# Buffers of the seven-product units in the place of the norms' tiles, half of the residual added on VectorE, and a finish without GpSimd

## The chip, the cores and the metric

The kernel runs on one core of a Trainium2 chip. The engines of the core work side by side, each in its own program order: TensorE multiplies (PE for the matmuls, PEld for its weight loads), VectorE (DVE), ScalarE (ACT) and GpSimd (POOL) work on tiles, and SyncE (SP) issues most of the transfers (DMA). An engine waits at an instruction until what that instruction needs is there, and everything behind it waits as well. The metric is the time of one execution on the device, in microseconds (us).

## The reference, cut to what matters

One layer of a trunk over 512 rows of 2048 values: normalise, project, mix, project back, add; then a feed-forward part with a convolution and a gate, and add again. What the change touches is the second and the third line.

```python
mixed = concatenate([y_sb, y_df, y_lru, y_sc], axis=-1) @ w_out[l]
x = x + rms_norm(mixed, norm_gains[l, 1])
h = rms_norm(x, norm_gains[l, 2])
u = causal_dwconv(h @ w_up, conv_w)          # three taps along the rows
g, up = split(u, 2, axis=-1)                 # 4096 columns each
x = x + rms_norm((gelu(g) * up) @ w_down, norm_gains[l, 3])
```

## The kernel before

Everything lies transposed: 128 partitions of columns, and the 512 rows run along the free axis in two halves of 256. Every float32 operand is split into a high and a low part, and a product is the sum of three (high by high, high by low, low by high). A weight tile of 128x1024 (512 KB) is loaded on SP's queue into a `w_raw` buffer, cast to `w_hi` on ACT, and its remainder `w_lo` is formed on DVE. That is `chunk` (lines 97 to 100) for the plain products, and `raw` (L993) with `operand` (L999, L1000) for the units below. TensorE needs one such tile about every 2.9 us.

The stages up to about 710 us (the input projection and the four mixers) are not touched. Then come:

- **The output projection** (`out_group`). Its last two groups of columns are worked for each half of the rows, first half 0, then half 1. When the last group of a half is done, `residual(hf)` is called a few ticks later. A tick is a piece of some four to eight matmuls, and `at` hangs work on a later tick.
- **`residual(hf)`** multiplies the projected values in `mg` by the norm's factor in eight operations on DVE (L833), and lets GpSimd add them to `x` with four transfers that accumulate in place (L834, `xs<-mg`, 512 KB each, q = 0 to 3).
- **`squares(hf, q)`** squares the new x on ACT (L844), sums on DVE (L846), writes the values scaled by the gains (L848) and stores x for later on SP's queue (L850, `x1_d`). Hung on ticks 22, 25, 28 and 31 after the residual; `norm2` on tick 42.
- **`norm2(hf)`** sums over the partitions with two matmuls on TensorE (L857, they read `s` from L846), and normalises and splits the result.
- **`up_plain`**: the first four pairs of column blocks of the up projection as plain products, each 128x514 row buffer `ub` (zeroed in its first two columns, L926) filled from PSUM, then convolved (`conv`: L939 on ACT, two taps L941 on DVE, into an `f2` tile) and gated (`glu`, L949).
- **`up_unit`**, 28 units (4 to 31), from about 865 to 1427 us. Each makes one pair of blocks from seven products instead of eight (a Strassen-like scheme): `product` (L1013 high, L1018 low) multiplies eight tiles of 128x512 and eight of 128x256. Sums of weight blocks are made by accumulating transfers of GpSimd (L1033), or on DVE in unit 4 (`add`, L1005). `keep` (L1028 on ACT, L1029 on DVE) and `add_result` (L1024) move PSUM results into `ug` and `uv`, the unit's two `ub` buffers. A PSUM tile is free for its next product when `keep` has read it.
- **The down projection**, and **`finish(hf)`** for each half: eight pairs of a multiplication by the factor (L1133) and an addition of the stored x (L1135). For half 1 four of the eight additions are on GpSimd, whose results leave by ACT's queue; the rest leaves by SP's.

Buffers: the pool `ph2` holds the norms' tiles; `t2f` has six `f2` tiles and `ubp` eight `ub` tiles, and all units share them with `up_plain`. The order of each engine's instructions is set by a scheduler; work under `high_priority` is put ahead of what stands later in the program.

Of the kernel before, what the change touches and what calls it, by code (L numbers as in the profile page):

```python
# [9 lines left out]
F32 = mybir.dt.float32  # L10
# [6 lines left out]
P = 128  # L17
# [31 lines left out]
def trunk(ctx: ExitStack, tc: tile.TileContext, xT, params, consts, wgate, w_in, w_out, w_up0, w_up, w_dn, out):  # L49
# [57 lines left out]
    def at(block, fn):  # L107
        assert block >= clock[0], (block, clock[0])
        beside.setdefault(block, []).append(fn)
# [662 lines left out]
    with ExitStack() as ph:  # L772
        wide = ph.enter_context(tc.tile_pool(name="wide", bufs=2))
        ystage = ph.enter_context(tc.tile_pool(name="ystage", bufs=3))
        up_ph = ph.enter_context(ExitStack())
        ph2 = up_ph.enter_context(tc.tile_pool(name="ph2", bufs=1))
        t2p = up_ph.enter_context(tc.tile_pool(name="t2f", bufs=6))
        ubp = up_ph.enter_context(tc.tile_pool(name="ubp", bufs=8))

        def t2(dt=F32):  # L780
            return t2p.tile([P, S], dt, name="f2")
# [43 lines left out]
        def residual(hf):  # L825

            ts = HALVES[hf]
            ss1[hf].rstd(rstd1[:, ts])
            acc = ph2.tile([P, 2, S // 2], F32, name="s2")
            for q in range(4):  # L830
                for i in range(2):
                    m = mg[q][hf][:, 2 * i:2 * i + 2]
                    V.tensor_tensor(out=m, in0=m, in1=repeated(rstd1[:, ts], 2), op=ALU.mult)  # L833
                G.dma_start(out=xs[q][hf], in_=mg[q][hf], accum_op=ALU.add)  # L834
                at(clock[0] + 22 + 3 * q, lambda q=q: squares(hf, q, acc))
            at(clock[0] + 42, lambda: norm2(hf, acc))

        def squares(hf, q, acc):

# [12 lines left out]
        def norm2(hf, acc):  # L852

            ts = HALVES[hf]
            ps = mm_tile()[:, 0:S // 2]
            for i in range(2):
                T.matmul(ps, lhsT=ones, rhs=acc[:, i], start=i == 0, stop=i == 1)  # L857
            with tc.high_priority(offset=AHEAD):
                rstd_of(ps, D, rstd2[:, ts], t1)
            for k in range(0, KT, 2):  # L860
                ks = slice(k % 4, k % 4 + 2)
                h = mg[k // 4][hf][:, ks]
                V.tensor_tensor(out=h, in0=h, in1=repeated(rstd2[:, ts], 2), op=ALU.mult)
                split(h, actq[k // 4][:, 0, ks, ts], actq[k // 4][:, 1, ks, ts])
            if hf == 1:
                sums_of_h()
# [59 lines left out]
            V.memset(t[:, 0:2], 0.0)  # L926
            return t

        neg_w = ph2.tile([P, 96], F32, name="neg_w")
        fw = PC["ffn_w"]  # L930
        V.tensor_scalar(out=neg_w, in0=par[:, fw + 96:fw + 192], scalar1=-1.0, scalar2=0.0,
                        op0=ALU.mult, op1=ALU.add)
# [42 lines left out]


        split_t2()
        spare_t = wide.tile([P, 4, 4, S // 2], F32, name="mg")
        spare = [spare_t[:, i] for i in range(4)]
        turn = [0]  # L980
# [7 lines left out]
        def up_unit(unit):  # L988
# [51 lines left out]


            a11, a21 = raw(spare[n], 0, 0), raw(spare[2 + n], 1, 0)
            s3, a12, a22 = (by4(wp.tile([P, 2, S], F32, name="w_raw")) for _ in range(3))
            s1 = a21
            if unit == 4:
                add(s3, a11, a21)
# [77 lines left out]
        def finish(hf):  # L1124
            ts = HALVES[hf]
            ss3[hf].rstd(rstd3[:, ts])
            for n in range(KT // 2):
                ks = slice(2 * (n % 2), 2 * (n % 2) + 2)
                t = m3[n // 2][:, ks, ts]
                x1 = t2() if n % 2 == 0 else ystage.tile([P, S], F32, name="ys")  # L1130
                x1 = x1.rearrange("p (k t) -> p k t", k=2)
                nc.sync.dma_start(out=x1, in_=x1_d[n // 2][:, hf, ks])
                V.tensor_tensor(out=t, in0=t, in1=repeated(rstd3[:, ts], 2), op=ALU.mult)  # L1133
                pool = hf == 1 and n in (1, 3, 5, 6)
                (G if pool else V).tensor_tensor(out=x1, in0=t, in1=x1, op=ALU.add)  # L1135
                (nc.scalar if pool else nc.sync).dma_start(out=out[hf, n], in_=x1)

        for g in range(3):
            down_group(g, (0, 1), ALL, mm_tile if g % 2 == 0 else pa_tile)
# [113 lines left out]
```

## Time and profile before

| | before |
|---|---|
| median of 3 runs | 1803.43 us (1801.49 to 1803.82) |
| the profiled execution | 1803.49 us, of which the trace's span is 1801.8 |
| TensorE busy | 1754.5 us, 97% |
| VectorE busy | 1152.3 us, 64% |
| ScalarE busy | 868.9 us, 48% |
| GpSimd busy | 151.0 us, 8% |
| mean granted clock of TensorE | 0.989 |

TensorE is busy nearly everywhere, so what can be gained lies in the few places where it isn't: they are read from its timeline, where an idle stretch stands in brackets with the engine and the tile that ended it. Busy is not the same as fast: after a long pause the granted clock falls, and the same instructions take longer.

### The profile page before, as it was taken

What the parts mean: (1) busy time and instruction counts of PE and PEld (TensorE: products, weight loads), DVE (VectorE), ACT (ScalarE), POOL (GpSimd) and SP (SyncE); (2) the same over time, 40 slices, a digit from 0 to 9 for tenths busy, and PEclk for the clock granted to TensorE, in tenths of its full rate; (3) what the DMA queues carried; (4) which work ended last, traced back from release to release, by engine and by line L of the source; (5) the groups of instructions that cost most, each with busy time, mean ns of one, the idle gap of its engine ahead of it and who ended that gap; (6) DMA issues with size and microseconds to landing.
All of it is one profiled execution on the core that took longest, in us unless ns stands there. A gap on an engine that the chain in (4) does not pass through costs nothing.

```text
span 1801.8 us, 24904 instructions
## 1 busy us (share of the span) xinstructions
PE 1754.5 (97%) x9612; PEld 1524.1 (85%) x9612; DVE 1152.3 (64%) x1716; ACT 868.9 (48%) x1301; POOL 151.0 (8%) x215
## 2 busy tenths in 40 slices
PE   8999999999999999999799999999999999999995
PEld 7778788887888889999788888888888888888995
DVE  7884576566656224679888888888788852222364
ACT  6442676655334335667455455555555642122342
POOL 0000011100000111100011111111111001010101
PEclk9999999999999999999899999999999999999998
DMA  7224222242222635875788888888897773233465
GB/s 258 82 97 141 78 77 77 88 152 82 94 94 89 202 106 176 245 235 186 221 219 237 228 218 234 232 226 230 228 232 208 233 234 94 93 102 98 130 212 172
DMA packets 95726, 299.21 MB, mean 166 GB/s; under 512 B 10324, under 2 KB 14676, under 8 KB 95608
## 3 DMA queue, kind: packets, MB, share of 16 engines
q1 hardware_dynamic: 82072, 249.39, 42.3%
q0 software_dynamic: 12960, 47.19, 14.0%
q8 instruction: 75, 1.23, 0.3%
q10 hardware_dynamic: 576, 1.05, 0.2%
q14 instruction: 43, 0.35, 0.1%
HBM read 258.78 MB, written 21.24 MB: 155 GB/s over the span
## 4 chain that ended last, share of the span: by engine, by line
PE 90%; DVE 3%; issue 3%; DMA 2%; ACT 1%; POOL 0%; SPq 0%; ACTq 0%; POOLq 0%; DVEq 0%
PE mm L150 41%; PE mm L1013 20%; PE mm L1018 10%; PE pa L150 9%; PE mm L121 2%; PE mm L123 2%; PE mm L122 2%; PE pa L575 1%; DMA w_raw<-in_w_out_dram 1%; DMA xs<-mg 1%; DMA w_raw<-in_w_up_dram 1%; DVE f L941 1%; PE pa L680 0%; DVE vd L267 0%; DVE w_lo L100 0%
## 5 line engine op out<-in xcount | busy, mean ns | idle before, releaser
L100 DVE TENSOR_TENSOR w_lo<-w_raw,w_hi 128x1024 fp32r<-128x1024 f32 (+1 forms) x249 | 305.0, 1226 | 401.4 <-PE mm L150 187.7
L99 ACT CAST w_hi<-w_raw 128x1024 fp32r<-128x1024 f32 (+1 forms) x249 | 260.4, 1047 | 437.1 <-PE mm L150 287.8
L150 PE MATMUL mm<-a,w_hi 128*128 128x512 f32 (+1 forms) x2048 | 433.0, 362 | 2.8 <-DVE t L318 2.1
L150 PEld LDWEIGHTS mm<-a,w_hi 128*128 128x128 f32 x2048 | 347.7, 189 | 61.3 <-DVE t L318 2.6
L1013 PE MATMUL mm<-a,w_hi 128*128 128x512 f32 x896 | 227.3, 396 | 9.7 <-DVE ub L926 6.4
L150 PE MATMUL mm<-a,w_lo 128*128 128x512 f32 (+1 forms) x1024 | 230.8, 364 | 0.0
L150 PEld LDWEIGHTS mm<-a,w_lo 128*128 128x128 f32 x1024 | 173.1, 190 | 28.0 <-issue 1.5
L999 ACT CAST w_hi<-w_raw 128x1024 fp32r<-128x1024 f32 x112 | 117.5, 1049 | 163.3 <-PE mm L1013 130.6
L1013 PEld LDWEIGHTS mm<-a,w_hi 128*128 128x128 f32 x896 | 162.6, 191 | 39.6 <-DVE ub L926 6.6
L1000 DVE TENSOR_TENSOR w_lo<-w_raw,w_hi 128x1024 fp32r<-128x1024 f32 x112 | 136.8, 1221 | 39.6 <-ACT w_hi L999 39.6
L1018 PEld LDWEIGHTS mm<-a,w_lo 128*128 128x128 f32 x896 | 123.9, 193 | 9.0
L999 ACT CAST w_hi<-mg 128x1024 fp32r<-128x1024 f32 x84 | 87.6, 1044 | 85.3 <-PE mm L1013 82.8
L1018 PE MATMUL mm<-a,w_lo 128*128 128x256 f32 x896 | 126.4, 284 | 0.0
L1000 DVE TENSOR_TENSOR w_lo<-mg,w_hi 128x1024 fp32r<-128x1024 f32 x84 | 102.5, 1220 | 22.7 <-ACT w_hi L999 22.7
L150 PE MATMUL pa<-a,w_hi 128*128 128x256 f32 (+1 forms) x704 | 107.1, 306 | 6.9 <-ACT w_hi L99 6.9
L1013 PE MATMUL mm<-xs,w_hi 128*128 128x512 f32 x448 | 112.4, 393 | 0.0
L150 PEld LDWEIGHTS pa<-a,w_hi 128*128 128x128 f32 x704 | 97.2, 194 | 12.5 <-ACT w_hi L99 7.4
L1013 PEld LDWEIGHTS mm<-xs,w_hi 128*128 128x128 f32 x448 | 80.5, 189 | 14.5
L1024 DVE TENSOR_TENSOR ub<-ub,mm 128x256 f32<-128x256 f32 x168 | 69.8, 415 | 34.5 <-PE mm L1018 34.4
L799 POOL TENSOR_TENSOR ss<-ss,q 128x256 f32<-128x256 f32 x49 | 37.9, 793 | 339.8 <-ACT q L795 338.9
L1018 PEld LDWEIGHTS mm<-xs,w_lo 128*128 128x128 f32 x448 | 61.1, 190 | 4.4
L1018 PE MATMUL mm<-xs,w_lo 128*128 128x256 f32 x448 | 62.5, 282 | 0.0
(269 smaller groups left out, 2464.2 us busy)
## 6 DMA issues: line engine op xcount, KB each, us to landing
w_raw<-in_w_up_dram SPq DMA_DIRECT2D x115, 512.0 KB, 5.3
w_raw<-in_w_in_dram SPq DMA_DIRECT2D x87, 512.0 KB, 3.5
w_raw<-in_w_dn_dram SPq DMA_DIRECT2D x80, 512.0 KB, 3.5
mg<-in_w_up_dram SPq DMA_DIRECT2D x56, 512.0 KB, 4.3
w_raw<-in_w_out_dram SPq DMA_DIRECT2D x48, 512.0 KB, 3.5
w_raw<-mg POOLq DMA_DIRECT2D x28, 512.0 KB, 5.7
mg<-in_w_up_dram POOLq DMA_DIRECT2D x27, 512.0 KB, 8.0
w_raw<-in_w_up_dram POOLq DMA_DIRECT2D x27, 512.0 KB, 9.3
```

The source lines that it names most:

```text
L99: w_split.append(A.copy(out=hi[:, sl], in_=raw[:, sl]))
L100: V.tensor_tensor(out=lo[:, sl], in0=raw[:, sl], in1=hi[:, sl].bitcast(F32), op=ALU.subtract)
L121: T.matmul(ps, lhsT=sh, rhs=mh, start=first, stop=False)
L122: T.matmul(ps, lhsT=sh, rhs=ml, start=False, stop=False)
L123: T.matmul(ps, lhsT=sl, rhs=mh, start=False, stop=last)
L150: T.matmul(pss[u], lhsT=a, rhs=b, start=c == 0 and kk == 0 and not low and i == 0, stop=False)
L799: G.tensor_tensor(out=self.acc, in0=self.first if self.n == 1 else self.acc, in1=sq, op=ALU.add)
L999: w_split.append(A.copy(out=by4(hi), in_=v))
L1000: V.tensor_tensor(out=by4(lo), in0=v, in1=by4(hi).bitcast(F32), op=ALU.subtract)
L1013: T.matmul(ps.rearrange("p (a t) -> p a t", a=2), lhsT=hi[:, k * P:(k + 1) * P], rhs=tops[name][k], start=first and k == 0, stop=False, **kw)
L1018: T.matmul(ps[:, 0:256], lhsT=lo[:, k * P:(k + 1) * P], rhs=tops[name][k][:, 0], start=False, stop=k == 7, **kw)
L1024: V.tensor_tensor(out=t, in0=t, in1=part, op=ALU.add)
```

## The change

- Units 4 to 31 get pools of their own, `t2s` (four `f2` tiles) and `ubs` (four `ub` tiles), in the space of the norms' tiles: `ph2` now has an exit of its own, after `split_t2()`. `up_plain` keeps its six and eight. `neg_w` moves into a small pool of its own.
- In `residual` only q = 0 and 1 are added by GpSimd's transfers; q = 2 and 3 are added by DVE, four operations of 128x512 per half. `squares` and `norm2` are hung two ticks earlier.
- In `up_unit` the tile `a12` is taken from the `w_raw` pool before `s3`.
- In `finish` all additions are on DVE, and every second output tile, of both halves, leaves by ACT's queue.

```diff
+        neg_p = up_ph.enter_context(tc.tile_pool(name="neg_p", bufs=1))
-        ph2 = up_ph.enter_context(tc.tile_pool(name="ph2", bufs=1))
         t2p = up_ph.enter_context(tc.tile_pool(name="t2f", bufs=6))
         ubp = up_ph.enter_context(tc.tile_pool(name="ubp", bufs=8))
+        norm_ph = up_ph.enter_context(ExitStack())
+        ph2 = norm_ph.enter_context(tc.tile_pool(name="ph2", bufs=1))
...
                     V.tensor_tensor(out=m, in0=m, in1=repeated(rstd1[:, ts], 2), op=ALU.mult)
-                G.dma_start(out=xs[q][hf], in_=mg[q][hf], accum_op=ALU.add)
-                at(clock[0] + 22 + 3 * q, lambda q=q: squares(hf, q, acc))
-            at(clock[0] + 42, lambda: norm2(hf, acc))
+                if q < 2:
+                    G.dma_start(out=xs[q][hf], in_=mg[q][hf], accum_op=ALU.add)
+            for q in range(2, 4):
+                for i in range(2):
+                    m, x = (t[q][hf][:, 2 * i:2 * i + 2] for t in (mg, xs))
+                    V.tensor_tensor(out=x, in0=x, in1=m, op=ALU.add)
+            for q in range(4):
+                at(clock[0] + 20 + 3 * q, lambda q=q: squares(hf, q, acc))
+            at(clock[0] + 40, lambda: norm2(hf, acc))
...
         split_t2()
+        norm_ph.close()
+        t2p = up_ph.enter_context(tc.tile_pool(name="t2s", bufs=4))
+        ubp = up_ph.enter_context(tc.tile_pool(name="ubs", bufs=4))
...
-            s3, a12, a22 = (by4(wp.tile([P, 2, S], F32, name="w_raw")) for _ in range(3))
+            a12, s3, a22 = (by4(wp.tile([P, 2, S], F32, name="w_raw")) for _ in range(3))
...
-                pool = hf == 1 and n in (1, 3, 5, 6)
-                (G if pool else V).tensor_tensor(out=x1, in0=t, in1=x1, op=ALU.add)
-                (nc.scalar if pool else nc.sync).dma_start(out=out[hf, n], in_=x1)
+                V.tensor_tensor(out=x1, in0=t, in1=x1, op=ALU.add)
+                (nc.scalar if n % 2 else nc.sync).dma_start(out=out[hf, n], in_=x1)
```

How the instructions stand is shown at three places. First VectorE at the end of `residual` for half 0, before (`s` is the running sum of squares that `norm2` reads):

```order
L833 TENSOR_TENSOR mg<-mg,rstd_4754 128x512 x3
L846 TENSOR_TENSOR s_5890<-s_5890,f_6066 128x512
L100 TENSOR_TENSOR w_lo<-w_raw,w_hi 128x1024
L846 TENSOR_TENSOR s_5890<-s_5890,f_6104 128x512
L100 TENSOR_TENSOR w_lo<-w_raw,w_hi 128x1024
L846 TENSOR_TENSOR s_5890<-s_5890,f_6107 128x512
```

and the same place after (L836 is the old L833, L855 the old L846):

```order
L836 TENSOR_TENSOR mg<-mg,rstd_4757 128x512 x3
L842 TENSOR_TENSOR xs<-xs,mg 128x512
L100 TENSOR_TENSOR w_lo<-w_raw,w_hi 128x1024
L842 TENSOR_TENSOR xs<-xs,mg 128x512 x2
L100 TENSOR_TENSOR w_lo<-w_raw,w_hi 128x1024
L842 TENSOR_TENSOR xs<-xs,mg 128x512
L855 TENSOR_TENSOR s_5893<-s_5893,f_6059 128x512
L855 TENSOR_TENSOR s_5893<-s_5893,f_6083 128x512
```

The four additions stand directly behind the multiplications, ahead of every sum of squares. Second, TensorE at `norm2` of half 0, both orders in one piece of the difference (L866 is the old L857, the other rows are products of the group):

```order
-L150 MATMUL pa<-a_80,w_hi 128x256 x16
-L150 MATMUL pa<-a_80,w_lo 128x256 x4
-L857 MATMUL mm<-s_5890,con 128x256 x2
-L150 MATMUL pa<-a_80,w_lo 128x256 x4
+L150 MATMUL pa<-a_80,w_hi 128x256 x8
+L866 MATMUL mm<-s_5893,con 128x256 x2
+L150 MATMUL pa<-a_80,w_hi 128x256 x8
+L150 MATMUL pa<-a_80,w_lo 128x256 x8
```

The two matmuls that read `s` stand twelve matmuls earlier in their chunk. Half 1 has the same move. Third, VectorE late in unit 4, before (`ub_7636` is unit 4's `uv`, `mm_7639` the PSUM tile of its fourth product, `ub_7634` its `ug`, and the `f2` tiles 7610 and 7623 belong to the last two blocks of `up_plain`):

```order
L941 SCALAR_TENSOR_TENSOR f2_7623<-ub_7086,par_74,f2_7623 128x512
L941 SCALAR_TENSOR_TENSOR f2_7610<-ub_7077,par_74,f2_7610 128x512
L1000 TENSOR_TENSOR w_lo_7834<-mg_7633,w_hi_7833 128x1024
L949 TENSOR_TENSOR f2_7610<-f2_7610,f2_7340 128x512
L1005 TENSOR_TENSOR mg_7633<-mg_7633 128x1024
L941 SCALAR_TENSOR_TENSOR f2_7623<-ub_7086,par_74,f2_7623 128x512
L926 MEMSET ub_7634 128x2
L926 MEMSET ub_7636 128x2
L949 TENSOR_TENSOR f2_7623<-f2_7623,f2_7352 128x512
L1029 TENSOR_TENSOR ub_7636<-ub_7636,mm_7639 128x256
```

and after (`ub_7650` is `uv`, `mm_7653` the same PSUM tile, L1041 the old L1029, L1012 the old L1000):

```order
L1041 TENSOR_TENSOR ub_7648<-ub_7648,mm_7652 128x256
L1012 TENSOR_TENSOR w_lo_7759<-w_raw_7657,w_hi_7758 128x1024
L950 SCALAR_TENSOR_TENSOR f2_7617<-ub_7084,par_74,f2_7617 128x512
L1041 TENSOR_TENSOR ub_7650<-ub_7650,mm_7653 128x256
L1012 TENSOR_TENSOR w_lo_7781<-w_raw_7659,w_hi_7780 128x1024
L950 SCALAR_TENSOR_TENSOR f2_7617<-ub_7084,par_74,f2_7617 128x512
L950 SCALAR_TENSOR_TENSOR f2_7630<-ub_7093,par_74,f2_7630 128x512
```

The instruction that frees the fourth product's PSUM tile has moved ahead of the taps and the gating of the last plain blocks, and of one remainder split; the memsets of the unit's row buffers stand some twenty rows earlier.

## Rows read from the trace of the kernel before

**Rows 1.** Windows: from:to and length, PE, PEld, DVE, ACT, POOL busy, PEclk, DMA share, GB/s.
```profile
850.00:895.00 45.00, 35.31 (x219) 32.13 (x219) 38.90 (x56) 22.18 (x31) 3.50 (x4) 0.90 0.78 230
895.00:1425.00 530.00, 529.97 (x3034) 466.35 (x3033) 436.87 (x673) 278.20 (x385) 67.90 (x78) 1.00 0.85 224
```

**Rows 2.** Timeline, PE, both output halves: start, duration, instruction, [idle before it, what ended it].
```profile
741.66 2.94 PE L150 MATMUL pa<-a,w_hi 128*128 128x256 f32 x16 [3.45 <-ACT w_hi L99]
...
799.51 2.81 PE L150 MATMUL pa<-a,w_hi 128*128 128x256 f32 x16 [3.40 <-ACT w_hi L99]
```

**Rows 3.** Timeline of PE in units 4 and 5.
```profile
871.54 3.04 PE L1013 MATMUL mm<-a,w_hi 128*128 128x512 f32 x8 [3.29 <-ACT w_hi L999]
874.38 1.77 PE L1018 MATMUL mm<-a,w_lo 128*128 128x256 f32 x8
875.99 2.00 PE L1013 MATMUL mm<-a,w_hi 128*128 128x512 f32 x8
877.83 1.11 PE L1018 MATMUL mm<-a,w_lo 128*128 128x256 f32 x8
...
891.02 3.78 PE L1013 MATMUL mm<-a,w_hi 128*128 128x512 f32 x8 [6.40 <-DVE ub L926]
894.60 1.89 PE L1018 MATMUL mm<-a,w_lo 128*128 128x256 f32 x8
```

**Rows 4.** The accumulating transfers: line L834, and their queue between 715 and 760 us.
```profile
DMA to landing us min/median/max: 5.7/9.4/12.4
```
```profile
q0 software_dynamic: 576, 2.10, 25.5%
```

**Rows 5.** Timelines of POOL and of SP's queue in half 0.
```profile
726.26 0.86 POOL L834 DMA_DIRECT2D xs<-mg  x1 [1.46 <-DVE mg L833]
...
742.86 4.01 POOL L799 TENSOR_TENSOR ss<-ss,q 128x256 f32<-128x256 f32 x4 [14.13 <-ACT q L795]
```
```profile
736.49 0.33 SPq L850 DMA_DIRECT2D x_d<-xs  x1
736.91 6.31 SPq L98 DMA_DIRECT2D w_raw<-in_w_out_dram  x2
```

**Rows 6.** Timeline of ACT: four rows of half 0 and 1, one of unit 4.
```profile
733.60 1.70 ACT L848 ACTIVATE mg<-xs,par 128x256 f32<-128x256 f32 x4
740.57 1.04 ACT L99 CAST w_hi<-w_raw 128x1024 fp32r<-128x1024 f32 x1 [5.27 <-DMA w_raw<-in_w_out_dram]
...
750.00 0.67 ACT L844 ACTIVATE f<-xs 128x512 f32<-128x512 f32 x1
...
798.41 1.04 ACT L99 CAST w_hi<-w_raw 128x1024 fp32r<-128x1024 f32 x1 [3.27 <-DMA w_raw<-in_w_up_dram]
...
870.45 1.04 ACT L999 CAST w_hi<-w_raw 128x1024 fp32r<-128x1024 f32 x1 [1.79 <-DMA w_raw<-in_w_up_dram]
```

**Rows 7.** Timeline of DVE in half 0, and in units 4 and 5.
```profile
741.64 1.22 DVE L100 TENSOR_TENSOR w_lo<-w_raw,w_hi 128x1024 fp32r<-128x1024 f32 x1 [6.62 <-ACT w_hi L99]
...
743.96 0.69 DVE L846 TENSOR_TENSOR s<-s,f 128x512 f32<-128x512 f32 x1 [0.49 <-ACT f L844]
...
889.86 0.07 DVE L926 MEMSET ub<- 128x2 f32 x2
...
890.55 0.41 DVE L1029 TENSOR_TENSOR ub<-ub,mm 128x256 f32<-128x256 f32 x1
...
904.53 0.74 DVE L941 SCALAR_TENSOR_TENSOR f<-ub,neg_w,f 128x512 f32<-128x512 f32 x1
```

**Rows 8.** Timeline of the end: DVE and SP.
```profile
1786.78 1.29 DVE L1133 TENSOR_TENSOR m<-m,rstd 128x512 f32<-128x512 f32 x2
...
1788.60 2.35 DVE L1133 TENSOR_TENSOR m<-m,rstd 128x512 f32<-128x512 f32 x2
...
1796.78 1.58 DVE L1135 TENSOR_TENSOR ys<-m,ys 128x512 f32<-128x512 f32 x1
...
1798.38 0.34 SPq L1136 DMA_DIRECT2D out_dram<-ys  x1
```

More of the change, by code (lines that the diff above doesn't have):

```diff
@@ L927, in up_tile @@
             return t
-        neg_w = ph2.tile([P, 96], F32, name="neg_w")
+        neg_w = neg_p.tile([P, 96], F32, name="neg_w")
         fw = PC["ffn_w"]
```

## The prediction

> **What bounds the kernel now.** I read the share of busy time by engine first, then a table of windows by stage, then TensorE's timeline in the windows where it is not full, and at each pause the timeline of the engine named in the brackets. TensorE is busy 97% of the span, and from 895 to 1425 us, where 27 of the 28 units run, it is busy for 529.97 of 530 us [rows 1]. Nothing can be gained there. What is left in the stretches that the change touches is four pauses and the end:
>
> - one in each half of the output projection, 3.45 and 3.40 us, both ended by a cast on ACT [rows 2];
> - two in unit 4, 3.29 us ended by a cast and 6.40 us ended by VectorE [rows 3]; the window around them holds 35.31 us of work in 45 us and a clock of 0.90 [rows 1];
> - the end, where VectorE and GpSimd finish the second half's output after TensorE has stopped [rows 8].
>
> Each pause costs more than its length, because the product behind it runs slowly. Behind the 3.29 us its two halves took 3.04 and 1.77 us where the next product's took 2.00 and 1.11: 1.70 us more. Behind the 6.40 us they took 3.78 and 1.89, that is 2.56 us more [rows 3]. The first matmuls behind the pauses of the output projection are drawn out alike (2.94 and 2.81 us) [rows 2], so I charge 1.7 us to each. With that the four cost 5.15, 5.10, 4.99 and 8.96 us.
>
> **The change part by part.** *Output projection, half 0.* The cast that ended the pause waited 5.27 us for a weight tile [rows 6]. Its load was issued on SP at 736.91, directly behind a store of x at 736.49 [rows 5]. That store waits for the third accumulating transfer, issued at 726.26 [rows 5], 10.2 us earlier; the eight transfers took 5.7 to 12.4 us to land [rows 4]. So the chain is: transfer, store, load queued behind the store, cast, matmul. The transfers also fill the engines that carry the loads: four of them took 25.5% of 45 us [rows 4], 2.9 us of all sixteen engines each. The change takes the third and the fourth of four out of that chain. In their place stand four VectorE additions of the shape that took 0.69 us [rows 7], 2.8 us together, directly behind the multiplications. They are hidden: VectorE then waits 6.62 us for the same late cast [rows 7]. If that cover were gone they would cost 2.8 us once per half. The third store can go at about 731 instead of 736.5, and its load with it; the pause goes.
>
> What is late next is the sum for `norm2`, whose two matmuls stand twelve matmuls earlier now. A matmul of 256 columns costs 0.12 us (eight of 512 columns start 1.84 us before what follows them) [rows 3]. TensorE, without the pause, would start the chunk of 741.66 at 738.2 and reach `norm2` after 56 matmuls, 6.7 us later: 744.9. ACT had finished the second q's work at 735.3; from the late cast at 740.57 to the end of the last square at 750.67 it had 10.1 us of work [rows 6], which can now follow at once: 745.4. With one addition on VectorE behind it (0.69) [rows 7] the sum is there at 746.1. TensorE would then wait some 1.2 us, which may cost 1.7 us of slow clock as well. Gain: 5.15, less 1.2 = 4.0 us; 2.3 if the clock falls, 5.2 if ACT is quicker.
>
> A rule speaks against the sum of squares staying at 0.69 us: four additions of GpSimd ran from 742.86 to 746.87 [rows 5], and VectorE's sum at 743.96 took 0.69 us beside them [rows 7], no longer. The Trainium skill, "SBUF — State Buffer", section "Who interferes with whom", says that a VectorE operation with two inputs in SBUF and a GpSimd operation that reads SBUF share a read port, and that whichever is issued later waits for the whole of the other. This trace agrees only at the end of the kernel, where two multiplications take 1.29 us alone and 2.35 beside GpSimd [rows 8]. By the rule one sum would be 1.06 us later and this half would gain about 3.0; by the row it is not, and I go by the row.
>
> *Output projection, half 1.* The same chain, cast at 798.41 behind 3.27 us of waiting for a tile [rows 6]. Here VectorE's chain runs earlier against the squares, and nothing of half 1's sum is later than TensorE: gain 5.0 us. Low end 2.0: half the pause stays and the clock falls as before.
>
> *Unit 4, the first pause.* The cast at 870.45 waits for a weight tile (`a12`) [rows 6] which SP issues last of six loads. The new allocation order of `a12` and `s3` leaves SP's order as it is, so `a12` still lands behind the others. Only two things move it: the chain of `norm2` starts 1.44 us earlier in TensorE's work (12 by 0.12), and one tap more (0.74) [rows 7] stands ahead of the operation that frees the loads' buffers. Net 0.7 us earlier. Gain 0.7; bounds 0 and 4.99.
>
> *Unit 4, the second pause.* TensorE asks for the fourth product's PSUM tile at 884.6 (891.02 less 6.40). The addition that frees it ran on VectorE only at 890.55, behind two memsets at 889.86 [rows 7] and, by the order shown with the change, behind taps and gatings of the plain blocks and one remainder split. With the units' own row buffers and convolution tiles the scheduler puts it ahead of all of these. It then needs the copy on ACT and its own 0.41 us [rows 7]; I leave 1.5 us of the wait for these and for small waits that the displaced taps cause later, no slow clock. Gain 8.96 - 1.5 = 7.4. The taps, gatings and the split are not gone, only later: they compete in unit 5, where the window around it has VectorE busy for 38.90 of 45 us [rows 1]. Low end: 3 us of waiting stay with 1.7 of slow clock, gain 4.3. High end 8.96.
>
> *The units after it.* Four row buffers instead of eight, two per unit. A pair was zeroed at 889.86 and its last tap ended at 905.27 [rows 7], 15.4 us; with four it is wanted again two units later, 39 us at 530/27 = 19.6 us a unit [rows 1]. Cost nothing. Bounds: 0, and the rival below.
>
> *The end.* The multiplication pairs run 1.29 us alone, and 2.35 us when GpSimd adds beside them; the last addition takes 1.58 us and ends at 1798.36 [rows 8]. With sixteen operations on VectorE alone at 0.61 to 0.645 us from 1786.78, it ends at 1796.5 to 1797.1. Gain 1.3 to 1.8, taken as 1.6; nothing, if the reloads of x are the next to wait. Half 0's stores on ACT's queue are issues between casts, beside a full TensorE: nothing.
>
> Sum: 4.0 + 5.0 + 0.7 + 7.4 + 1.6 = 18.7 us. Against the profiled execution (1803.49, span 1801.8, 1.7 outside; 0.06 above the median) that is **1784.8 us**. All good ends: 5.2 + 5.1 + 4.99 + 8.96 + 1.8 = 26, 1777. All poor ends: 2.3 + 2.0 + 0 + 4.3 + 0 = 8.6, 1795.
>
> **The rivals.** *The transfers stay the bound in the output projection.* Two accumulating transfers of 2.9 us each remain per half, loads land late behind them all the same, and only unit 4 and the end pay: 0.7 + 7.4 + 1.6 = 9.7, 1793.8. For it: the first two transfers carry the first two stores. Against: the load that was late was behind the third.
>
> *VectorE becomes the bound in units 4 and 5.* The displaced taps come back as a wait a few products later: 4.3 instead of 7.4 and, with the sum of `norm2` late and a slow clock in half 0, 2.3 instead of 4.0: 1789.9. For it: 38.90 of 45 us [rows 1].
>
> *The change doesn't do what it says in unit 4*: `a12` and the loads behind it set the pace there, and a freed PSUM tile only meets the next late tile. Then 4.0 + 5.0 + 1.6 = 10.6, and 1793.
>
> *Slower.* With half the row buffers and four of six convolution tiles, a unit's memset or first tap waits for the gating of an earlier one, and TensorE waits with it, in each of 28 units. The price is per unit: 18.7/28 = 0.67 us a unit eats the gain, and from 0.80 us the kernel is slower by over 0.2%; with 1.0 us it is 1813. For it: TensorE has no slack to hide anything in these units. Against: a pair is held 15.4 us of 39.
>
> **How the numbers follow.** The forecast, about 1781 to 1788.5, gets 0.55. Below it 0.08. The second rival and mixtures of it 0.17, the first and the third together 0.10: these end at 1788.5 to 1796. Same, most of the gains gone, 0.04. Slower 0.06. The predicted time is the forecast's, 1784.8. The range 1777 to 1796 takes in the sums of the good and poor ends and leaves about 0.12 out. About 0.2%, 3.6 us, is what a measurement of this kernel can tell from no change: faster by that 0.90, within it 0.04, slower 0.06.
>
> **What would show it.** TensorE's pauses at 741 and 799 us gone, with a wait of about 1 us for `s` in front of `norm2` in half 0 and none in half 1; the store of the third q on SP some 5 us earlier. In unit 4 a pause of 2.5 to 3.3 us still ended by a cast, and the 6.40 us one down to 1 or 2. From unit 6 to 31 TensorE as full as before: any pause ended by a memset, a tap or a gating there shows the rival that ends slower. At the end, multiplications of 0.68 us throughout. The forecast is wrong if weight tiles land late in the output projection with only two accumulating transfers, or if TensorE waits for VectorE in units 5 and 6 for more than 2 us.

## The result and the profile after

The changed kernel took 1787.32 us (median of 4 runs, 1785.91 to 1790.58), the kernel before 1802.46 in the same set of runs: a ratio of 0.9919 with a 95% interval of 0.9902 to 0.9936, 15.1 us less. The forecast was 18.7 us less. In a later set the changed kernel took 1788.35 us (6 runs) against 1801.6, ratio 0.9924 (0.9907 to 0.9940). The profiled execution took 1785.91 us, with this head of its page:

```profile
span 1784.2 us, 24937 instructions
...
PE 1747.6 (98%) x9612; PEld 1518.6 (85%) x9612; DVE 1155.5 (65%) x1728; ACT 868.9 (49%) x1301; POOL 142.1 (8%) x207
```

TensorE does the same 9612 matmuls in 7 us less of busy time: what has gone from its busy time is slow clock, 2 us of it in the stretch up to 727 us that no part of the change touches.

Since the number of matmuls is the same, the starts of the n-th matmul in two executions can be compared, and the time that a stage gained or lost read off. Below it is so for every profiled execution of this study, each against the profiled execution before. The first column is a stretch that no part of the change touches.

| us against before | up to 727 (untouched) | output half 0 | output half 1, up_plain | units 4 to 6 | behind the last matmul |
|---|---|---|---|---|---|
| forecast | 0 | -4.0 | -5.0 | -8.1 | -1.6 |
| changed kernel | -2.1 | -4.0 | -3.8 | -6.6 | -1.1 |
| the same again (e10) | -0.5 | -3.8 | -4.3 | -6.1 | -1.1 |
| e1 pools alone | -2.7 | -0.3 | +0.9 | -2.5 | -0.1 |
| e2 residual alone | -2.2 | -2.3 | -2.3 | -4.5 | -0.1 |
| e3 finish alone | +0.3 | -0.1 | -0.5 | +0.3 | -1.1 |
| e4 a12 first | +0.4 | -2.9 | -4.1 | -2.2 | -1.1 |
| e5 unit 4's loads first | -1.2 | -1.8 | -3.8 | -6.1 | -1.0 |
| e6 ticks back | +0.1 | -5.1 | -3.8 | -0.9 | -1.2 |
| e7 two row buffers | +0.6 | -2.6 | -4.2 | -2.8 | -1.1 |
| e8 ticks alone | +0.6 | +0.9 | +2.4 | -4.1 | 0.0 |
| e11 late g | +0.2 | -3.5 | -4.2 | -6.0 | -1.0 |
| e12 both | +0.2 | -2.3 | -5.1 | -9.5 | -1.1 |
| e13 squares earlier | -2.7 | -4.0 | -4.2 | -9.3 | -1.1 |

The four touched stages gave 15.5 us in the profiled execution. That fits the 15.1 us of the medians, while the 2.1 us in the untouched stretch are an accident of that execution (below). From unit 7 to the last matmul all executions take the same time, 0.37 us less than the one of the kernel before; these 0.37 us are in the column of units 4 to 6, whatever the kernel.

**The output projection.** TensorE's timeline of the changed kernel has these pauses left, where [rows 2] had 3.45 and 3.40 us:

```profile
744.50 1.13 PE L866 MATMUL mm<-s,con 128*128 128x256 f32 x4 [1.71 <-DVE s L855]
...
790.47 2.18 PE L150 MATMUL pa<-a,w_hi 128*128 128x256 f32 x16 [0.47 <-ACT w_hi L99]
...
794.88 1.13 PE L866 MATMUL mm<-s,con 128*128 128x256 f32 x4 [0.31 <-DVE s L855]
```

The cast's late weight tile is gone, and half 0 waits for the sum instead. SP's timeline shows why the tile is no longer late; the third store is the second of these rows, behind the second by 1.15 us where [rows 5] had it waiting for a transfer:

```profile
729.36 0.33 SPq L859 DMA_DIRECT2D x_d<-xs  x1
...
730.51 0.62 SPq L859 DMA_DIRECT2D x_d<-xs  x1
```

The accumulating transfers, four now, landed in 5.5 to 8.5 us, median 6.6 (9.4 in [rows 4]).

**Units 4 and 5.** The rows that answer [rows 3], TensorE, and the cast on ACT that ends the first pause:

```profile
862.12 3.78 PE L1025 MATMUL mm<-a,w_hi 128*128 128x512 f32 x8 [3.81 <-ACT w_hi L1011]
865.70 1.91 PE L1030 MATMUL mm<-a,w_lo 128*128 128x256 f32 x8
...
888.44 2.14 PE L1025 MATMUL mm<-a,w_hi 128*128 128x512 f32 x8 [1.05 <-DVE ub L1041]
```
```profile
861.02 1.04 ACT L1011 CAST w_hi<-w_raw 128x1024 fp32r<-128x1024 f32 x1 [0.26 <-DMA w_raw<-in_w_up_dram]
```

The first pause, in front of unit 4's second product, has grown from 3.29 to 3.81 us, with a slow clock over the whole product behind it (granted clock 0.50). The second, 6.40 us in front of the sixth product, is gone; a wait of 1.05 us stands in front of unit 5's third product. The windows that answer [rows 1] (the same stretches of the program, 10 us earlier):

```profile
840.00:885.00 45.00, 41.19 (x261) 37.70 (x260) 39.68 (x54) 25.77 (x35) 4.25 (x5) 0.92 0.76 222
885.00:1415.00 530.00, 528.95 (x3025) 465.13 (x3024) 441.41 (x685) 280.38 (x388) 67.12 (x78) 1.00 0.86 228
```

TensorE works 41.19 us of 45 instead of 35.31. The long window shows the 1.05 us pause and nothing else: four row buffers and four convolution tiles cost the units nothing.

**The end.** The rows that answer [rows 8], of VectorE:

```profile
1770.28 1.29 DVE L1145 TENSOR_TENSOR m<-m,rstd 128x512 f32<-128x512 f32 x2
...
1778.98 0.69 DVE L1146 TENSOR_TENSOR f<-m,f 128x512 f32<-128x512 f32 x1 [0.19 <-DMA f<-x_d]
1780.31 0.69 DVE L1146 TENSOR_TENSOR ys<-m,ys 128x512 f32<-128x512 f32 x1 [0.64 <-DMA ys<-x_d]
```

No multiplication is drawn out (0.68 us each throughout), but the last two additions wait 0.83 us for reloads of x, which SP issued only at 1775.04 and 1775.52. Hence 1.1 us instead of 1.6.

### The profile page after: what moved, and what is told of

Same layout as the page of the kernel before. It is cut to its first block, busy times and chain, and to the rows that moved or that the text cites. A ratio compares the mean times of both kernels' runs of the same rounds, so it can differ in the third digit from the quotient of the medians.

```text
span 1784.2 us, 24937 instructions
## 1 busy us (share of the span) xinstructions
PE 1747.6 (98%) x9612; PEld 1518.6 (85%) x9612; DVE 1155.5 (65%) x1728; ACT 868.9 (49%) x1301; POOL 142.1 (8%) x207
## 4 chain that ended last, share of the span: by engine, by line
PE 91%; DVE 3%; DMA 3%; ACT 2%; issue 1%; SPq 0%; POOL 0%; POOLq 0%; DVEq 0%; ACTq 0%
PE mm L150 41%; PE mm L1025 20%; PE mm L1030 10%; PE pa L150 9%; PE mm L121 2%; PE mm L123 2%; PE mm L122 2%; PE pa L575 1%; DMA w_raw<-in_w_up_dram 1%; DMA xs<-mg 1%; DVE w_lo L100 1%; ACT w_hi L99 1%; PE pa L680 0%; DVE vd L267 0%; DVE w_lo L1012 0%
## 5 line engine op out<-in xcount | busy, mean ns | idle before, releaser
L1012 DVE TENSOR_TENSOR w_lo<-w_raw,w_hi 128x1024 fp32r<-128x1024 f32 x112 | 136.8, 1222 | 38.5 <-ACT w_hi L1011 37.0
L1012 DVE TENSOR_TENSOR w_lo<-mg,w_hi 128x1024 fp32r<-128x1024 f32 x84 | 102.6, 1221 | 25.3 <-ACT w_hi L1011 25.3
```

The lines of the kernel that those rows point to most:

```text
L1012: V.tensor_tensor(out=by4(lo), in0=v, in1=by4(hi).bitcast(F32), op=ALU.subtract)
```

## The experiments

**One part at a time.** e1 takes the pools part of the diff (with the order of `a12` and `s3`), e2 the residual part with its ticks, e3 the finish part, each on the kernel before.

```diff
# e1
...
+        t2p = up_ph.enter_context(tc.tile_pool(name="t2s", bufs=4))
+        ubp = up_ph.enter_context(tc.tile_pool(name="ubs", bufs=4))
# e2
+                if q < 2:
+                    G.dma_start(out=xs[q][hf], in_=mg[q][hf], accum_op=ALU.add)
...
+                    V.tensor_tensor(out=x, in0=x, in1=m, op=ALU.add)
...
+                at(clock[0] + 20 + 3 * q, lambda q=q: squares(hf, q, acc))
+            at(clock[0] + 40, lambda: norm2(hf, acc))
# e3
+                V.tensor_tensor(out=x1, in0=t, in1=x1, op=ALU.add)
+                (nc.scalar if n % 2 else nc.sync).dma_start(out=out[hf, n], in_=x1)
```

> The kernel before with the pools part alone: neg_w and the norms' tiles in pools of their own, four f2 and four ub tiles for units 4 to 31, a12 taken before s3. The residual, its ticks and the finish are those of before. Theory (each part acts in its own stretch, and the parts add up): the two pauses in the output projection (about 3.4 us each) and the end stay as they were, the 6.4 us pause of unit 4 falls to 1 to 2 us, so about 7.5 us less than before, give or take what the first pause of unit 4 does (3.3 us before, 3.8 us after). Rival (the pools alone don't reorder VectorE, the earlier norm2 does): the 6.4 us pause stays and the time is that of before within 2 us.

Measured: 1801.62 us against 1801.89, ratio 0.9998 (0.9989 to 1.0007): no difference that the medians show. The theory fell, and the rival held: the long pause of unit 4 is still there, in TensorE's timeline:

```profile
887.75 3.59 PE L1019 MATMUL mm<-a,w_hi 128*128 128x512 f32 x8 [5.78 <-DVE ub L929]
```

and VectorE's order there is that of before: two memsets and the last taps and gatings stand ahead of the addition that frees the fourth product. The stage gained 2.5 us in the profiled execution, which was the fastest of eleven (1798.86 us); the medians show none of it.

> The kernel before with the residual part alone: q = 2 and 3 added on VectorE, squares and norm2 two ticks earlier. Theory: the pauses of 3.4 us in both halves go, a wait of 1 to 2 us for the sum stays in half 0; 7.8 us less than before; unit 4 keeps its two pauses. Rival (freeing the output projection only makes unit 4 wait longer): the pauses of unit 4 grow by several us and the gain is below 4 us.

Measured: 1792.18 us, ratio 0.9947 (0.9934 to 0.9961), 9.7 us less. The theory was right on the output projection in kind, but the gain there was short of its size (4.6 instead of 7.8 us), and it was wrong on unit 4, which gained 4.5 us without the pools. With this part alone VectorE's order in unit 4 is already that of the changed kernel. What the pools add on top of it shows in one row of TensorE and one of ACT:

```profile
893.71 2.11 PE L1019 MATMUL mm<-a,w_hi 128*128 128x512 f32 x8 [3.06 <-DVE ub L1035]
```
```profile
890.40 0.72 ACT L945 ACTIVATE f<-ub,neg_w 128x512 f32<-128x512 f32 x1 [1.72 <-DMA g_d<-f]
```

The first tap of unit 4's second block waits 1.72 us for an `f2` tile that is still being stored, and behind it on ACT stand a cast and the copy out of the next PSUM tile. e8 below has the same wait (1.73 us) and a pause of 3.10 us. With four tiles of the units' own this wait isn't there, and the pause was 1.05, 1.81 and 1.91 us in the three executions with the changed kernel's order here (the changed kernel twice, and e11).

> The kernel before with the finish part alone: all additions on VectorE, every second output tile on ACT's queue. Theory: about 1.1 us less, all of it behind TensorE's last matmul, since the last two reloads of x wait for their buffers. Rival (the stores of half 0 on ACT's queue hold up casts): a pause of TensorE in the last 60 us and no gain.

Measured: 1801.93 us, ratio 0.9995 (0.9986 to 1.0004), which can't tell 1.1 us from nothing; the last column of the table shows it, the same 1.0 to 1.2 us in every kernel that has this part and 0.0 to 0.1 in those without. No pause of TensorE came with it in its last stage, so the rival fell.

**What moved VectorE's order in unit 4.** e6 takes the two ticks back in the changed kernel, e8 makes them the only edit of the kernel before.

```diff
# e6, on the changed kernel
-                at(clock[0] + 20 + 3 * q, lambda q=q: squares(hf, q, acc))
-            at(clock[0] + 40, lambda: norm2(hf, acc))
+                at(clock[0] + 22 + 3 * q, lambda q=q: squares(hf, q, acc))
+            at(clock[0] + 42, lambda: norm2(hf, acc))
# e8, on the kernel before
-                at(clock[0] + 22 + 3 * q, lambda q=q: squares(hf, q, acc))
-            at(clock[0] + 42, lambda: norm2(hf, acc))
+                at(clock[0] + 20 + 3 * q, lambda q=q: squares(hf, q, acc))
+            at(clock[0] + 40, lambda: norm2(hf, acc))
```

> The changed kernel with squares and norm2 hung on the ticks of the kernel before (22 + 3q and 42). The additions on VectorE, the new pools and the finish stay. Theory (the two ticks, not the pools and not the additions, move the freeing of the fourth product ahead of the taps on VectorE): the order of the instructions has the late place again, and the 5 to 6 us pause with a slow clock is back in unit 4, 5 to 7 us more than the changed kernel, while half 0's wait of 1.7 us for the sum shrinks to under 0.5. Net 1791 to 1794. Rival (that place isn't what the pause hangs on): unit 4 stays at about 1 us of waiting, and the time falls below the changed kernel's by the 1.3 us in half 0.

Measured: 1791.44 us, ratio 0.9943 (0.9930 to 0.9955). TensorE's timeline has both things that the theory wanted, the short wait and the long pause:

```profile
747.04 1.13 PE L866 MATMUL mm<-s,con 128*128 128x256 f32 x4 [0.55 <-DVE s L855]
```
```profile
882.56 3.68 PE L1025 MATMUL mm<-a,w_hi 128*128 128x512 f32 x8 [5.25 <-DVE ub L935]
```

Units 4 to 6 lose 5.7 of the 6.6 us, half 0 gains 1.1; by the medians 9.9 us are left of the 13.3 to 15.1. So in the changed kernel, pools and additions left as they are, the ticks are worth 5 to 6 us in a stage that runs some 100 us later.

> The kernel before with nothing but the two numbers changed: squares and norm2 hung two ticks earlier. All four quarters are still added by transfers, pools and finish are those of before. Theory (the ticks alone move the freeing of the fourth product forward): unit 4's 6.4 us pause falls to about 3 us as with the whole residual part, the 3.4 us pauses of the output projection stay or grow by up to 1.4 us of waiting for the sum: 2 to 5 us less than before. Rival (the additions on VectorE are needed for it): the time of before, within 2 us, with the long pause still there.

Measured: 1801.36 us, ratio 0.9995 (0.9986 to 1.0003). The units gain 4.1 us, as in e2, and VectorE's order there is the early one; the output projection loses 3.3 us. In half 0 (0.9 us) the late tiles stay and a wait of 1.78 us for the sum comes on top; in half 1 (2.4 us) the pause for the late tile has grown to 4.27 us, with a slow clock behind it. The sum is nothing. The theory held in kind in both stages, but the output projection lost more than the 1.4 us that it allowed for; the total was at the rival's number for another reason. In the order of the instructions alone (no run was made of it), one tick more for `norm2` (41, with the squares where they are) brings the late place back: it is the tick of `norm2` that the scheduler's choice turns on. That of the squares turns nothing, as e13 shows below.

**The first pause of unit 4.** e4 issues `a12` ahead of everything else of unit 4; e5 leaves unit 4's order and puts unit 5's first two loads behind it.

```diff
# e4
+            if unit == 4:
+                a12 = by4(wp.tile([P, 2, S], F32, name="w_raw"))
+                raw(a12, 0, 1)
...
             a11, a21 = raw(spare[n], 0, 0), raw(spare[2 + n], 1, 0)
# e5
+            def raw_after(t, a, b):
+                with tc.high_priority(offset=AHEAD), tc.issue_after(last_of_4[0]):
...
+            first_two = raw_after if unit == 5 else raw
+            a11, a21 = first_two(spare[n], 0, 0), first_two(spare[2 + n], 1, 0)
```

> The changed kernel, and in unit 4 the load of a12 is issued first, ahead of the four loads of units 4 and 5 and of a22. Theory (unit 4's first pause is the landing of a12 behind five other loads): the pause of 3.8 us and the 2.6 us of slow clock behind it go, 4 to 6.4 us less than the changed kernel, about 1781 to 1783. Rival (VectorE is the bound there, by its taps): the cast runs early, but the pause is now ended by VectorE's w_lo or by the PSUM tile of the first product, and less than 2 us are gained.

Measured: 1791.84 us, ratio 0.9949 (0.9937 to 0.9962): not faster than the changed kernel, some 4 us slower. The second product ran without a pause, so `a12` was what it had waited for. But the third waited, for a cast that waits for VectorE's sum of three blocks. One of these (`a22`) is now the last to be issued, but VectorE shows no gap there in which it waits for it: it works on from 850 us, with taps ahead of the sum. And the edit brought back the late order around the fourth product. TensorE, then ACT:

```profile
866.93 3.48 PE L1025 MATMUL mm<-a,w_hi 128*128 128x512 f32 x8 [2.50 <-ACT w_hi L1011]
...
883.04 3.78 PE L1025 MATMUL mm<-a,w_hi 128*128 128x512 f32 x8 [5.89 <-DVE ub L1041]
```
```profile
865.84 1.99 ACT L1011 CAST w_hi<-mg 128x1024 fp32r<-128x1024 f32 x2 [3.30 <-DVE mg L1017]
```

The rival held, and a second thing neither had: the order.

> The changed kernel, with unit 5's first two weight loads issued behind unit 4's last one, so that a22 and a12 of unit 4 come third and fourth on SP's queue instead of fifth and sixth. VectorE's order around the fourth product stays the changed kernel's. Theory (unit 4's first pause is a12's place in the queue): a12 lands about 3 us earlier, the pause falls from 3.8 to about 1 us and the slow clock behind it (2.6 us) goes: 4 to 5.5 us less than the changed kernel, about 1782 to 1783. Rival (the sums on VectorE set the pace there, as with a12 alone issued first): the pause moves to the third product and under 1.5 us are gained.

Measured: 1790.46 us, ratio 0.9942 (0.9930 to 0.9954); no gain over the changed kernel. Unit 4 has three short pauses now, of 0.69, 1.45 and 1.11 us, none with a slow clock behind it, and by the end of unit 5 the stage was 10.1 us ahead of before; then 4 us of that were lost again in unit 6:

```profile
911.59 2.10 PE L1031 MATMUL mm<-a,w_hi 128*128 128x512 f32 x8 [3.50 <-DVE ub L1047]
```
```profile
903.91 1.05 ACT L1017 CAST w_hi<-w_raw 128x1024 fp32r<-128x1024 f32 x1 [7.47 <-DMA w_raw<-in_w_up_dram]
```

That cast's tile was issued on SP at 897.20, behind a reload of g (for the down projection, 500 us later) that stood at the head of SP's queue until the store of the same tile had landed. SP issued nothing between the load before, at 891.66, and that reload:

```profile
891.66 0.37 SPq L1006 DMA_DIRECT2D w_raw<-in_w_up_dram  x1
896.31 0.33 SPq L1127 DMA_DIRECT2D ys<-g_d  x1
```

The reload is only one reason for the total: half 0 gained 1.8 us here instead of 4.0, for a reason that the edit doesn't touch (see e13).

**Five hundred microseconds early.** e11 and e12 put these reloads behind the loads of unit 20, on the changed kernel and on e5; e10 is the changed kernel beside them.

```diff
...
                     y = ystage.tile([P, S], F32, name="ys")
-                    nc.sync.dma_start(out=y, in_=g_d[4 * n + i])
+                    with tc.issue_after(w_load[first_load[20]].ins):
+                        nc.sync.dma_start(out=y, in_=g_d[4 * n + i])
```

> The changed kernel once more, unchanged, beside the two that follow and the kernel before. By its first profile: 1785 to 1790, 12 to 16 us less than before. Theory (a pause of a given length is followed by a slow clock in some executions and not in others): the pauses stand at the same places with lengths within half a microsecond, and differences of 1 to 2.6 us per pause between this execution and the first come from the matmuls behind them. Rival (the order of arrival of transfers differs): the pauses' own lengths differ by more than 1 us.

Measured: 1788.35 us. The pauses stand at the same places, 1.78, 3.90 and 1.81 us where the first execution had 1.71, 3.81 and 1.05; half 1's pause of 0.47 us is not there. Two of the lengths differ by 0.5 to 0.8 us, a little more than the theory allowed and less than the rival's 1 us.

> The changed kernel, with the first three reloads of g for the down projection (which the scheduler puts between the weight loads of units 4 to 6) issued behind the loads of unit 20. Theory (unit 4's first pause is a12's place in the queue, and no reload is ahead of it): no difference, within 1 us of the changed kernel. Rival (the reloads hold weight loads up behind them, as each waits for the store of the same tile): 1 to 4 us less.

Measured: 1788.19 us, no difference from e10. In the changed kernel nothing waits behind the reloads.

> Both edits: unit 5's first loads behind unit 4's last, and the early reloads of g behind the loads of unit 20. Theory (with unit 4's first pause gone, the next late thing was a weight load of unit 6 queued on SP behind a reload that waits for its store, which held it up by 4 us): the 3.5 us pause of unit 6 goes as well; unit 4's two pauses shrink to about 1 us each, 5 to 6 us less than the changed kernel, about 1781 to 1783. Rival (VectorE's load is the bound in units 4 to 6): a wait of 2 to 4 us ended by VectorE comes back a few products later, and under 2 us are gained.

Measured: 1785.80 us (5 runs, 1785.41 to 1787.74), ratio 0.9912 (0.9897 to 0.9926) against 0.9924 (0.9907 to 0.9940) for the changed kernel beside it. The intervals overlap, so the medians don't settle these 2.5 us; the stage does, with 9.5 us gained in units 4 to 6 (9.3 in e13) against 6.1 and 6.6. TensorE's pauses there:

```profile
861.79 2.11 PE L1031 MATMUL mm<-a,w_hi 128*128 128x512 f32 x8 [0.65 <-ACT w_hi L1017]
...
865.33 1.22 PE L1036 MATMUL mm<-a,w_lo 128*128 128x256 f32 x8 [1.43 <-DVE w_lo L1018]
...
872.34 2.11 PE L1031 MATMUL mm<-xs,w_hi 128*128 128x512 f32 x8 [0.21 <-DVE ub L1047]
```

In these units each edit alone was worth nothing, both together some 3 us. That is short of the theory's 5 to 6. Six pauses of 0.19 to 1.43 us are left in units 4 to 6, and five of them, 2.40 of 3.05 us, are ended by VectorE; but in e13, where the order is the same, the longest (1.71 us) is ended by the cast again. What sets them stays open.

**Half 0's wait for the sum**, on e12: the squares two ticks earlier.

```diff
-                at(clock[0] + 20 + 3 * q, lambda q=q: squares(hf, q, acc))
+                at(clock[0] + 18 + 3 * q, lambda q=q: squares(hf, q, acc))
```

> The kernel of e12 with squares hung two ticks earlier still (18 + 3q), norm2 where it is (40), so that VectorE's order in unit 4 stays the early one. Theory (norm2 of half 0 waits 1.8 us for the last squares on ACT, which stand behind casts and copies): with the squares ahead of some of these the sum is there 0.5 to 1.5 us earlier, and the time falls by 1 to 3 us, about 1783 to 1785. Rival (ACT is busy without a gap from the first landing on, and the first two quarters come no earlier): the wait stays, or a cast that was put off makes a pause of its own; no gain, within 1 us of e12.

Measured: 1785.99 us, ratio 0.9912 (0.9895 to 0.9928), the same as e12. The wait stays at 1.72 us. But the edit moved nothing: in the traces of e12 and e13 every engine has the same instructions in the same order. So neither the theory nor the rival was tested, and what the wait would cost to remove stays open. What speaks for the rival is ACT's timeline in e13, which has no idle stretch over 0.15 us between 724.90 and 745.07.

As a second execution of e12's order, e13 is worth having. The rows are `norm2` of half 0 in e5, e12 and e13; the same four matmuls take 1.13 us behind one wait and 2.07 and 1.99 behind the others, in which the slow clock went on for the next product and cost the half about 2 us:

```profile
746.08 2.07 PE L866 MATMUL mm<-s,con 128*128 128x256 f32 x4 [2.29 <-DVE s L855]
```
```profile
746.96 1.99 PE L866 MATMUL mm<-s,con 128*128 128x256 f32 x4 [1.76 <-DVE s L855]
```
```profile
743.93 1.13 PE L866 MATMUL mm<-s,con 128*128 128x256 f32 x4 [1.72 <-DVE s L855]
```

**Fewer row buffers**, the case in which the change would have been slower, driven further:

```diff
-        ubp = up_ph.enter_context(tc.tile_pool(name="ubs", bufs=4))
+        ubp = up_ph.enter_context(tc.tile_pool(name="ubs", bufs=2))
```

> The changed kernel with two row buffers for units 4 to 31 instead of four, so that a unit can't start its pair before the last taps of the unit ahead. Theory (a pair is held some 15 to 16 us of the 19.6 us of a unit): a slack of about 4 us is left, and the units cost 0 to 0.3 us each: at most 8 us more than the changed kernel. Rival (the slower case of the forecast, row buffers bound the units): a wait of 1 us or more in each of 28 units, over 28 us more than the changed kernel, ended by a memset, a tap or a row buffer's copy.

Measured: 1793.38 us, ratio 0.9954 (0.9942 to 0.9966), 5 to 6 us more than the changed kernel. Most of it is one pause in unit 5, where a copy on ACT waits for the taps of unit 4, which come late. With the slow product behind it, it cost 6.0 us, where the pause at the same place cost 1.3 and 2.1 us in the two executions of the changed kernel. The rest lies in half 0, which the edit doesn't touch. The window over the later units is full. TensorE, ACT, and the window:

```profile
894.29 3.52 PE L1025 MATMUL mm<-a,w_hi 128*128 128x512 f32 x8 [4.39 <-DVE ub L1041]
```
```profile
892.85 0.37 ACT L1040 COPY ub<-mm 128x256 f32<-128x256 f32 x1 [2.30 <-DVE f L950]
```
```profile
900.00:1420.00 520.00, 520.00 (x2978) 457.48 (x2977) 429.55 (x668) 274.34 (x378) 66.31 (x76) 1.00 0.85 225
```

So even two would do from unit 6 on; the buffers matter at the seam between the plain blocks and the units.

## Why the prediction was right, and where its reasons were not

The time, the direction and the range held. Point by point:

- **Output projection, half 0** (forecast 4.0, measured 4.0 and 3.8). Right in mechanism: the store that waited for the third transfer, the load queued behind it, and the wait for the sum that takes their place. That wait was 1.71 us instead of 1.2, without the slow clock that I had left open. That the size came out is in part luck. Nine profiled executions have this order of instructions in half 0 (the changed kernel twice, e2, e4, e5, e7, e11, e12, e13); it gained 1.8 to 4.0 us in them, 3.0 in the mean. In e5 and e12 the slow clock did follow the wait, and the half gained 1.8 and 2.3, the 2.3 of the low end; in e2, e4 and e7 a wait of 0.65 to 1.38 us for a cast was there besides. The rule on the shared read port, which I set aside for this place, does show: three sums took 2.98 us beside GpSimd's four additions, which took 5.19 us instead of the 4.01 of [rows 5]. The 4.01 were drawn out already: one of these additions takes 0.74 us in the median of its line, and 1.20 at most. The price was about the 1.06 us stated, but VectorE then waited 0.41 us for ACT, and the sum waits for the last squares on ACT, so nothing came of it in the time. The rows: VectorE, GpSimd, GpSimd's line in the kernel before (shortest, median and longest in ns), and ACT:

```profile
735.23 2.98 DVE L855 TENSOR_TENSOR s<-s,f 128x512 f32<-128x512 f32 x3
```
```profile
735.30 5.19 POOL L802 TENSOR_TENSOR ss<-ss,q 128x256 f32<-128x256 f32 x4 [12.64 <-ACT q L798]
```
```profile
L799 POOL TENSOR_TENSOR ss<-ss,q x49: 723/737/1201, 620.8 to 1782.0; 128x256 f32<-128x256 f32 x49
```
```profile
742.44 0.67 ACT L853 ACTIVATE f<-xs 128x512 f32<-128x512 f32 x1
```

  The Trainium skill, "SBUF — State Buffer", section "Who interferes with whom", states this contention; the trace agrees with it here, by the 2.98 and 5.19 us. It agreed in the kernel before too, where I had read it as silent: GpSimd's 1.20 us were spent beside VectorE's sums at 742.78 and 743.96, so there it was GpSimd that waited.
- **Output projection, half 1** (5.0; 3.8 and 4.3). The pause went. I had said that nothing of half 1's sum is late: a wait of 0.31 us for it stayed in both executions, and one of 0.47 for a cast in one. Mis-sized by about 1 us. In e12, which has neither wait, the stage gained 5.1.
- **Unit 4, first pause** (a gain of 0.7; a loss of 1.6). The wrong sign. The step that failed is "the chain of `norm2` starts 1.44 us earlier ... Net 0.7 us earlier". It did start earlier, but VectorE lost the lead again: besides the tap that I had counted, it now stands idle for 0.99 us inside the norm's own chain, where the order before had a remainder split, so the operation that frees the loads' buffers came 0.6 us later against TensorE. The pause became 3.81 us, and the clock fell over the whole product (3.78 and 1.91 us where 3.04 and 1.77 had stood). Of the 2.3 us that the forecast missed here, 1.2 are the pause's length and 1.1 the slower product. That `a12`'s place in SP's queue sets it was right, as e4 and e5 show.
- **Unit 4, second pause** (7.4; 7.8). The size was right, the reason was not; it came out because the ticks that do the work are part of the same change. The sentence that failed is "With the units' own row buffers and convolution tiles the scheduler puts it ahead of all of these." e1 has the buffers and the late order, e2 and e8 have the early order without the buffers, e6 has the buffers with the late order: the two ticks of `norm2` do it. They are worth about two thirds of the stage's gain (4.5 and 4.1 us in e2 and e8, of 6.6 and 6.1). What the buffers do is the other third: they take away a wait of ACT for an `f2` tile (1.72 us in e2), and the pause in unit 5 is 1.05 to 1.91 instead of 3.06 us.
- **The units after it** (0; 0 from unit 6 on, e7 with half as many row buffers 0 as well). Right; the slower rival had no ground.
- **The end** (1.6; 1.1). The mechanism was right; the reloads of x were the next to wait, 0.83 us, as the bound named.
- **The rival that VectorE becomes the bound in units 4 and 5** did not come at the price stated (which is 1789.6 by its own terms, not 1789.9), but the wait of 1.05 to 1.91 us in unit 5 is its beginning; a wait of more than 2 us there was to be the sign that the forecast is wrong.

In sum, 3.6 us were missing against the forecast in the profiled execution, the 0.37 us behind unit 6 left out: 2.3 in unit 4's first pause, 1.2 in half 1, 0.5 at the end, against 0.4 more in the second pause.

## What to carry to other kernels

When an edit moves a hint that a scheduler reads, look for what it moves far away: here two ticks of a hook that runs at 745 and 795 us were worth 5 to 6 us at 880, and the buffers that seemed to be the cause were not. Before a pause is put down to a part of a change, make each part alone and compare the order of the instructions at the pause. The same comparison tells whether an edit moves anything at all (e13 didn't). One profiled execution is a weak measure of a stage: the same order in half 0 gave 1.8 to 4.0 us. And where a pause has two things behind one another, an edit that removes the first is worth nothing until the second has gone too (by the stage, e5 and e11 alone nothing, together some 3 us).

## What was not expected of the hardware

That the clock falls after a long pause, as said ahead of the change, is not always so. The same pause is followed by a slow clock in one execution and not in another. In the untouched stretch, TensorE's timeline of the kernel before and of the changed kernel, with the same instructions and the same pause of 1.63 us:

```profile
208.95 0.85 PE L575 MATMUL pa<-t,tri_r 128*128 128x256 f32 x2 [1.63 <-ACT t L559]
...
209.81 3.32 PE L150 MATMUL mm<-a,w_hi 128*128 128x512 f32 x8
```
```profile
210.00 0.85 PE L575 MATMUL pa<-t,tri_r 128*128 128x256 f32 x2 [1.63 <-ACT t L559]
...
210.85 2.05 PE L150 MATMUL mm<-a,w_hi 128*128 128x512 f32 x8
```

Eight matmuls took 3.32 us before and 2.05 after, with a granted clock of 0.57 and 1.00 in these stretches, and the stretch cost 1.5 us more; the same happened once more at 425 us. Both together make 3.1 us, of which 1.0 had been lost in the first 12 us of the changed kernel's execution; that leaves the 2.1 of the table's first column. What decides it, no run here shows. The rows of the longer pauses say the same: 3.18 us of half 1 in e1 was followed by a first product of 3.79 us (granted clock 0.50), and 3.13 us of half 0 by one of 2.18 (1.00):

```profile
738.69 2.18 PE L150 MATMUL pa<-a,w_hi 128*128 128x256 f32 x16 [3.13 <-ACT w_hi L99]
...
743.22 2.18 PE L150 MATMUL pa<-a,w_hi 128*128 128x256 f32 x16 [1.40 <-ACT w_hi L99]
...
796.33 3.79 PE L150 MATMUL pa<-a,w_hi 128*128 128x256 f32 x16 [3.18 <-ACT w_hi L99]
```

The second of these rows also shows that a slow clock is not always a loss: where the clock stayed up, TensorE met the next cast 1.40 us before it was there. Charging each pause a fixed 1.7 us on top of its length, as the forecast did, fits the execution that it was read from and no other for certain. The pause in unit 5 was 3.06 us in e2, with eight matmuls in 2.11 us behind it, and 3.10 us in e8, with the same eight in 3.78:

```profile
902.27 3.78 PE L1013 MATMUL mm<-a,w_hi 128*128 128x512 f32 x8 [3.10 <-DVE ub L1029]
```
